# Retention values and gates of two heads as one 2x2 block product by seven products, with six blocks of branch gates made early and kept in DRAM

## The chip, the cores and the metric

One core of one Trainium2 chip runs the whole program. The metric is the time of one execution on the device in microseconds (us), median of several runs. TensorE is called PE here, VectorE DVE, ScalarE ACT, GpSimd POOL, and SyncE, whose queue issues every DMA of this kernel, SP.

## What is computed

Two layers of an encoder run over 512 tokens of width 1024. Each layer projects its input `x` by `w_in` into queries and keys of three branches, into values, into a retention gate and into three branch gates; mixes tokens by retention (A), chunked attention (B) and differential attention (C); adds the three branches under sigmoid gates; and ends with an output projection, a layer norm, a SwiGLU feed-forward part and a second norm.

```python
h = jnp.einsum('bsd,de->bse', x, w_in[l])
rq, rk, rv, rg, cq, ck, cv, dq, dk, dv, gates = jnp.split(h, splits, axis=-1)
o_a = _retention(rq, rk, rv, rg, ret_norm_g[l])
...
g = jax.nn.sigmoid(gates + b_merge[l]).reshape(B, S, N_BRANCHES, D)
merged = g[:, :, 0] * (o_a @ w_branch_a[l]) + g[:, :, 1] * (o_b @ w_branch_b[l]) + g[:, :, 2] * (o_c @ w_branch_c[l])
```

The change concerns `rv` and `rg` (1024 columns each, in two halves of 512 that serve two heads each) and `gates` (three branches of 1024 columns).

## The kernel before, in words

**Numbers.** Every float32 operand is held as a pair of float32r tiles, a high part and the remainder (`Pair`, `split`). A product of two such operands is three matmuls, high by high, high by low, low by high (`mm3`, L106 to L108). A weight block of 1 MB is loaded into a stage (`st`, three buffers), then ACT casts the high part (`wh`, L135) and DVE subtracts to get the low part (`wl`, L136), in two pieces each; there are three such pairs of weight buffers (`AHEAD`), so weights are prepared up to three blocks ahead of PE. All other tiles of 128x512 share one pool of 60 slots (`NSLOT`). [...]

**Order of the work.** A layer is a list of items, each a weight block (or some of them) and a function that issues its matmuls (L902 and on, and after it the output projection and the feed-forward items). `run_items` (L440) fetches weights ahead. Between the products of an item `between` (L434) issues steps of the attention branches: `s_r1` to `s_r3` for retention, `c(i)` (L887) for the chunked attention, `d(i)` for the differential attention. The framework then schedules the instructions of each engine into one static queue; an instruction waits at the head of its engine's queue for semaphores, and everything behind it waits with it.

**Start of a layer.** `u_first` (L562) projects the first queries and keys for retention. In the first layer (`whole`) eight tiles of x arrive one by one beside the first weight block, and 48 matmuls of two banks run in the order in which they arrive; then come two more weight blocks (96 matmuls). At its end it calls `vectors` (L491): seven small DMAs bring biases and norm weights as rows into one tile `rows`, PE transposes it into `pcol` (L503), ACT copies it to `colv`, and DVE makes `hb`, half the gate bias, from it. Before all this PE runs 16 transposes on the identity (L462).

**Values and gates.** `u_rv` (L555) and `u_rg` (L593) each take two weight blocks of 512 columns and make four token tiles in natural layout, `pn`, each by 8 k-tiles x 3 = 24 matmuls of 512 columns: 96 for `rv` and 96 for `rg` of one pair of heads. `u_gate(br, i)` (L855) makes two gate tiles (48 matmuls), ACT takes their tanh, and they stay in SBUF until the next item, `u_branch(br, i)` (L866), multiplies a branch's projection by them. The gates of branch A stand directly ahead of their branch, as do those of B; those of C are the last items ahead of C's branch.

**Feed-forward output.** Its first 16 k-tiles are done as 2x2 block products by seven products instead of eight (`Halves`, L142, loads and adds the weight blocks; `Quarters`, L212, the sums of the activations; `fout_items`, L1028), each product interleaved with a 48-matmul item of the feed-forward input.

**Norm.** At the end of a layer `Norm.to_T` (L405) makes the transposed input of the next one: ACT applies the norm's weights into a passing tile `lnt` (L414), and `split` makes the pair.

Of the kernel before, what the change touches and what calls it, by code (L numbers as in the profile page):

```python
# [43 lines left out]
NSLOT = 60  # L44
# [9 lines left out]
def trunk(ctx, tc, x_in, xT_in, w_in, ret_norm_g, da_norm_g, lq1, lk1, lq2, lk2, w_a, w_b, w_c, b_merge, w_out,  # L54
# [87 lines left out]
    class Halves:  # L142
# [6 lines left out]
        def __init__(self, w, r0, kh):  # L149
            self.w, self.r0, self.kh = w, r0, kh  # L150

        def load(self, i, j, tag="st", **kw):
            t = wst.tile([P, 2048], F32, tag=tag, name=tag, **kw)[:, :512 * self.kh]
            t = t.rearrange("p (k c) -> p k c", k=self.kh)
            r = P * (self.r0 + i * self.kh)
            nc.sync.dma_start(t, self.w[r:r + P * self.kh, 512 * j:512 * j + 512].rearrange("(k p) c -> p k c", p=P))
            return t
# [54 lines left out]
    class Quarters:  # L212
# [3 lines left out]
        def __init__(self, t1, t2, scale=None):  # L216
            a, b = slice(0, 256), slice(256, 512)
# [11 lines left out]
            self.use = {"m1": (q[:, a], q[:, b])}  # L229
            for names, pr in ((("m2", "h"), p2), (("y", "x"), p12), (("v", "g"), p43)):  # L230
                for name, sl in zip(names, (a, b)):
                    self.use[name] = (pr.hi[:, sl], pr.lo[:, sl])
# [119 lines left out]
    class Norm:  # L352


        def __init__(self, z, gcol, bcol, gam, bet, xT, dst):
            self.__dict__.update(z=z, gcol=gcol, bcol=bcol, gam=gam, bet=bet, xT=xT, dst=dst)
            self.st = [small.tile([P, 2, 6], F32, tag="bn", name="bn") for _ in range(NT)]
            self.banks = {}
# [46 lines left out]
        def to_T(self, hf, ks=range(KT)):  # L405
            cols = slice(256 * hf, 256 * hf + 256)
            for k in ks:
# [3 lines left out]
                if self.gcol is not None:  # L411
                    t = g(name="lnt")[:, :256]
                    gc, bc = self.gcol[:, k:k + 1], self.bcol[:, k:k + 1]
                    nc.scalar.activation(t, src, AF.Identity, scale=gc, bias=bc)  # L414
                    src = t
                split(self.xT[k], src, cols=cols)
# [47 lines left out]
    start = {}  # L464

    def load_x(k0, k1):
        for k in range(k0, k1):
            start[k] = g(name="xn")
            nc.sync.dma_start(start[k], xT_in[P * k:P * k + P])

    def split_x(k0, k1):
        for k in range(k0, k1):
            xTs[0][k] = Pair("xT")
            src, pr = start.pop(k), xTs[0][k]
# [3 lines left out]
    xTs = [[None] * KT for _ in range(DEPTH + 1)]  # L478
    hooks = {}

    def layer(l):
        lambda_init = 0.8 - 0.6 * math.exp(-0.3 * l)
        xT = xTs[l]
# [65 lines left out]
        def rv_part(hp, wts, t):  # L549
            ps = bank("pn")  # L550
            proj_N(xT, wts, t, ps)
            rv[hp, t] = Pair("rv")
            split(rv[hp, t], ps)

        def u_rv(hp):  # L555
            def fn(*wts):
                for t in range(NT):
                    rv_part(hp, wts, t)
                    between()
            return rows_of(W, RV + 512 * hp), fn  # L560

        def u_first():  # L562

            dst = [(rq, 0), (rk, 0), (rq, 2)]

            def whole(*wts):
                ret_tables()
                banks = [bank("pt") for _ in range(2)]
# [4 lines left out]
                for w, (d, h) in zip(wts, dst):  # L573
                    for j in range(2):
                        rqk_done(d, h + j, banks[j] if w is wts[0] else proj_T(xT, w, P * j))
                vectors()

            def halves(*wts):
                ret_tables()
                banks = [[bank("pt") for _ in range(2)] for _ in wts[:2]]  # L580
# [4 lines left out]
                for w, p, (d, h) in zip(wts, banks, dst):  # L585
                    for j in range(2):
                        rqk_done(d, h + j, proj_T(xT, w, P * j, ps=p[j], half=1))
                vectors()

            fn = whole if l == 0 else halves  # L590
            return [([wcols(c, 256)], KT) for c in (RQ, RK, RQ + 256)], fn

        def u_rg(hp):  # L593
            def fn(*wts):
                for t in range(NT):
                    ps = bank("pn")
                    proj_N(xT, wts, t, ps)
# [4 lines left out]
                    between()  # L602
            return rows_of(W, RG + 512 * hp), fn
# [250 lines left out]

        def u_gate(br, i):  # L855
            def fn(wt):
                for j in range(2):
                    d = 2 * i + j
                    ps = proj_T(xT, wt, P * j)
                    t = g(name="th")  # L860
                    nc.scalar.activation(t, ps, AF.Tanh, scale=0.5, bias=v["hb"][:, 8 * br + d:8 * br + d + 1])
                    th[br, d] = t
# [3 lines left out]
        def u_branch(br, i):  # L866
# [3 lines left out]
            def fn(wt):  # L870
                act = (oa, ob, oc)[br]
                for j in range(2):
                    d = 2 * i + j
                    ps = proj_T(act, wt, P * j, nk=nk)
                    t = th.pop((br, d))
# [25 lines left out]

# [293 lines left out]
```

## Time and profile before

| | |
|---|---|
| median of 3 runs | 1943.55 us (1943.06 to 1944.1) |
| the profiled execution's own time | 1943.5 us |
| its span, first to last instruction | 1941.7 us |
| mean granted clock of PE | 0.998 |
| PE busy | 1928.8 us (99%), 9346 matmuls |
| DVE busy | 1189.0 us (61%) |
| ACT busy | 846.2 us (44%) |
| DMA | 214 MB on the SP queue |

The 1.8 us between the span and the execution's own time lie outside the recorded instructions. A page of the profile gives busy times by engine, the span in 40 slices, the chain of work that ended last, and groups of instructions by source line with their mean duration. Durations of neighbouring matmuls overlap, as the array is a pipeline; what a matmul costs is the distance between the starts of two neighbours, which the timeline view shows.

### The profile page before, as it was taken

The numbers are of one execution on the slowest core, as the hardware profiler recorded it, in microseconds if no ns is written. First come the engines' busy times: TensorE is split into PE (matmuls) and PEld (weight loads), VectorE is DVE, ScalarE is ACT, GpSimd is POOL, SyncE is SP. The second block draws the span as 40 slices with busy tenths as digits, with TensorE's granted clock in tenths as the row PEclk, the third lists the DMA queues.
The fourth block names the chain that finished last, engine by engine and source line by source line (L and its number), as shares of the span: only waits on it lengthen the run. The fifth ranks groups of instructions, "written<-read, shape, count | busy, mean of one in ns | idle before, by whom it ended". The sixth has DMA issues, their size and how long they took to land. (4 is left out here: it accounts for less than half of the span.)

```text
span 1941.7 us, 23842 instructions
## 1 busy us (share of the span) xinstructions
PE 1928.8 (99%) x9346; PEld 1624.6 (84%) x9346; DVE 1189.0 (61%) x2022; ACT 846.2 (44%) x1511; POOL 44.4 (2%) x73
## 2 busy tenths in 40 slices
PE   9999999999999999999999999999999999999998
PEld 7888888888888888888898888888888888888886
DVE  7455556577556766656576545655775567675666
ACT  5334455466534333333254344555674343332330
POOL 0000000000000000000000000000000000000000
PEclk9999999999999999999999999999999999999999
DMA  7232332232244443434343223222221624444341
GB/s 256 94 102 66 99 102 88 70 98 77 66 160 123 131 152 114 146 107 141 122 163 99 76 87 103 79 90 87 87 87 44 207 76 152 131 151 131 102 130 50
DMA packets 228533, 215.78 MB, mean 111 GB/s; under 512 B 7118, under 2 KB 179268, under 8 KB 228420
## 3 DMA queue, kind: packets, MB, share of 16 engines
q1 hardware_dynamic: 228420, 214.26, 35.2%
q8 instruction: 73, 1.20, 0.3%
q14 instruction: 40, 0.33, 0.1%
HBM read 205.84 MB, written 8.39 MB: 110 GB/s over the span
## 5 line engine op out<-in xcount | busy, mean ns | idle before, releaser
L106 PE MATMUL pt<-xTh,wh 128*128 128x512 f32 (+1 forms) x1584 | 596.8, 377 | 1.2 <-ACT xTh L475 1.1
L107 PE MATMUL pt<-xTl,wh 128*128 128x512 f32 (+1 forms) x1584 | 593.8, 375 | 1.1 <-DVE xTl L476 1.1
L108 PE MATMUL pt<-xTh,wl 128*128 128x512 f32 (+1 forms) x1584 | 593.2, 375 | 0.0
L136 DVE TENSOR_TENSOR wl<-st,wh 128x1024 fp32r<-128x1024 f32 (+1 forms) x314 | 353.3, 1144 | 176.7 <-ACT wh L135 176.6
L135 ACT CAST wh<-st 128x1024 fp32r<-128x1024 f32 (+1 forms) x314 | 301.6, 989 | 324.6 <-PE pt L107 162.3
L107 PEld LDWEIGHTS pt<-xTl,wh 128*128 128x128 f32 x1584 | 298.7, 189 | 54.4 <-DVE xTl L476 2.3
L106 PEld LDWEIGHTS pt<-xTh,wh 128*128 128x128 f32 x1584 | 298.5, 189 | 54.4 <-ACT xTh L475 2.4
L108 PEld LDWEIGHTS pt<-xTh,wl 128*128 128x128 f32 x1584 | 298.4, 188 | 53.7
L106 PE MATMUL pn<-wh,xTh 128*128 128x512 f32 x384 | 150.8, 393 | 0.0
L107 PE MATMUL pn<-wl,xTh 128*128 128x512 f32 x384 | 149.6, 390 | 0.0
L108 PE MATMUL pn<-wh,xTl 128*128 128x512 f32 x384 | 149.6, 390 | 0.0
L985 DVE TENSOR_TENSOR fth<-fth,pt 128x512 f32<-128x512 f32 x44 | 30.2, 686 | 115.6 <-PE pt L108 115.6
L108 PEld LDWEIGHTS pn<-wh,xTl 128*128 128x128 f32 x384 | 72.1, 188 | 15.2
L106 PEld LDWEIGHTS pn<-wh,xTh 128*128 128x128 f32 x384 | 72.1, 188 | 14.2
L107 PEld LDWEIGHTS pn<-wl,xTh 128*128 128x128 f32 x384 | 72.2, 188 | 14.0
L983 ACT ACTIVATE fth<-pt 128x512 f32<-128x512 f32 x44 | 26.3, 599 | 124.4 <-PE pt L108 124.4
L271 ACT COPY sw<-pt 32x512 f32<-32x512 f32 (+1 forms) x96 | 55.7, 580 | 31.4 <-PE pt L108 30.1
L984 DVE SCALAR_TENSOR_TENSOR fth<-fth,pt 128x512 f32<-128x512 f32 x44 | 30.1, 683 | 58.9 <-ACT fth L983 58.9
L209 ACT CAST wh<-st 128x1024 fp32r<-128x1024 f32 x32 | 32.1, 1051 | 74.4 <-PE pt L107 74.4
L106 PE MATMUL pt<-oah,wh 128*128 128x512 f32 x128 | 50.9, 397 | 0.0
L108 PE MATMUL pt<-oah,wl 128*128 128x512 f32 x128 | 50.0, 390 | 0.0
L107 PE MATMUL pt<-oal,wh 128*128 128x512 f32 x128 | 49.9, 390 | 0.0
(232 smaller groups left out, 2979.3 us busy)
## 6 DMA issues: line engine op xcount, KB each, us to landing
st<-in_w_in SPq DMA_DIRECT2D x55, 1024.0 KB
st<-in_w_ffn_in SPq DMA_DIRECT2D x88, 512.0 KB
st<-in_w_ffn_out SPq DMA_DIRECT2D x28, 1024.0 KB
st<-in_w_in SPq DMA_DIRECT2D x32, 512.0 KB
st<-in_w_branch_a SPq DMA_DIRECT2D x8, 1024.0 KB
st<-in_w_out SPq DMA_DIRECT2D x8, 1024.0 KB
saved<-z SPq DMA_DIRECT2D x24, 256.0 KB
z<-saved SPq DMA_DIRECT2D x24, 256.0 KB
```

The source lines that it names most:

```text
L106: nc.tensor.matmul(ps, lh, rh, start=start, stop=False)
L107: nc.tensor.matmul(ps, lh, rl, start=False, stop=False)
L108: nc.tensor.matmul(ps, ll, rh, start=False, stop=stop)
L135: done = [nc.scalar.copy(self.hi[:, a:b], st[:, a:b]), nc.vector.tensor_sub(self.lo[:, a:b], st[:, a:b], f(self.hi[:, a:b]))]
L136: nc.vector.tensor_sub(self.lo[:, a:b], st[:, a:b], f(self.hi[:, a:b]))]
L209: nc.scalar.copy(self.hi[:, s], st[:, s])
L271: nc.scalar.copy(sw[half * b:half * b + half], ps[half * o:half * o + half])
L983: nc.scalar.activation(t, pg, AF.Tanh, scale=0.5)
L984: nc.vector.scalar_tensor_tensor(t, t, 1.0, pg, op0=ALU.add, op1=ALU.mult)
L985: nc.vector.tensor_mul(t, t, pu)
```

## The change

For each pair of heads, `rv` and `rg` together (512 tokens by 1024 columns, 1024 deep) become one 2x2 block product by seven products, in the manner of the feed-forward output: `u_rvg` makes seven items `m1`, `y`, `x`, `m2`, `v`, `g`, `h`, each of one weight block of 512x512 and 2 x 4 x 3 = 24 matmuls of 512 columns. Four of the seven weight blocks are sums or differences made by DVE (`t1` to `t4`), and DVE also adds the products together. The activations' sums need x in float32, so x's tiles (`xf`, in the second layer written by `to_T`) stay until `s_q` has made the sums of four k-pairs. `u_first` takes the first gate block of branch A in place of the second block of queries, so `vectors`, which gives the gate bias, moves ahead of the first matmuls in both layers. Six gate blocks (`EARLY`: all four of A, two of C) stand between the seven products, leave SBUF to DRAM tiles and come back in the branch items. The steps of retention and of chunked attention move to other places in the list; `c(i)` now falls into nearly every item from the first branch on. `NSLOT` is 61. The feed-forward's `Quarters` is split into `parts` and `sums`, and `t4` adds where it subtracted, with the sign moved to its user.

In the built program the counts change so: matmuls of 512 columns from 7464 to 7368, other PE instructions not at all; DVE gains 32 instructions of 256 columns, 72 of 512 and 56 of 1024; ACT gains 32 of 512 and 24 of 1024; SP gains 60 DMAs and 25.2 MB.

```diff
+EARLY = [(0, 0), (0, 1), (0, 2), (0, 3), (2, 0), (2, 1)]
+
+NSLOT = 61
...
-        def __init__(self, w, r0, kh):
-            self.w, self.r0, self.kh = w, r0, kh
+        def __init__(self, w, r0, kh, cols=(0, 512)):
+            self.w, self.r0, self.kh, self.cols = w, r0, kh, cols
...
-            b, a = self.load(1, 0), self.__dict__.pop("a")
-            for s in self.parts():
-                nc.vector.scalar_tensor_tensor(b[:, s], a[:, s], -1.0, b[:, s], op0=ALU.mult, op1=ALU.subtract)
+            b = self.load(1, 0)
+            self.add(b, self.__dict__.pop("a"))
...
+    def product(acts, name, j, wt):
+
+        ps, sl = bank("pf"), slice(P * j, P * j + P)
+        for k in range(wt.nk):
+            hi, lo = acts[k].use[name]
+            mm3(ps, hi[:, sl], lo[:, sl], wt.hi[:, k], wt.lo[:, k], k == 0, k == wt.nk - 1)
+        return ps
 
...
+        def sums(self, t1, t2, scale=None):
+            a, b = self.A, self.B
             sa, sb = g(name="sa"), g(name="sb")
             nc.vector.tensor_sub(sa[:, a], t1[:, b], t2[:, b])
             nc.vector.tensor_sub(sa[:, b], t1[:, a], sa[:, a])
             nc.vector.tensor_sub(sb[:, a], t2[:, a], sa[:, b])
             nc.vector.tensor_sub(sb[:, b], t1[:, b], t1[:, a])
-            q, p2, p12, p43 = g(F32R, "q11"), Pair("q2"), Pair("s12"), Pair("s43")
-            part_hi(q[:, a], t1[:, a], scale)
-            part_lo(q[:, b], t1[:, a], q[:, a], scale)
-            split(p2, t2, scale=scale)
...
+                    if k not in self.rows:
+                        self.rows[k] = g(name="xf")
+                    t = self.rows[k][:, cols]
...
+            def done(i, j, ps):
+                if (i, j) == (0, 0):
+                    xq.update({k: Quarters(xT[k], xT[k + 4]) for k in range(4)})
+                if i < 2:
+                    rqk_done((rq, rk)[i], j, ps)
+                else:
+                    gate_done(0, j, ps)
 
             def whole(*wts):
                 ret_tables()
+                vectors()
                 banks = [bank("pt") for _ in range(2)]
                 for k in range(KT):
                     for j in range(2):
                         a, c = xT[k], slice(P * j, P * j + P)
                         mm3(banks[j], wts[0].hi[:, k, c], wts[0].lo[:, k, c], a.hi, a.lo, k == 0, k == KT - 1)
-                for w, (d, h) in zip(wts, dst):
+                for i, w in enumerate(wts):
                     for j in range(2):
-                        rqk_done(d, h + j, banks[j] if w is wts[0] else proj_T(xT, w, P * j))
-                vectors()
+                        done(i, j, proj_T(xT, w, P * j) if i else banks[j])
 
             def halves(*wts):
                 ret_tables()
+                vectors()
                 banks = [[bank("pt") for _ in range(2)] for _ in wts[:2]]
                 proj_T_half0(xT, [(w, P * j, p[j]) for w, p in zip(wts, banks) for j in range(2)], {})
                 banks.append([bank("pt") for _ in range(2)])
                 proj_T_half0(xT, [(wts[2], P * j, banks[2][j]) for j in range(2)],
                              {2 * b: functools.partial(hooks[l], b) for b in range(4)})
-                for w, p, (d, h) in zip(wts, banks, dst):
+                for i, (w, p) in enumerate(zip(wts, banks)):
                     for j in range(2):
-                        rqk_done(d, h + j, proj_T(xT, w, P * j, ps=p[j], half=1))
-                vectors()
+                        done(i, j, proj_T(xT, w, P * j, ps=p[j], half=1))
 
             fn = whole if l == 0 else halves
-            return [([wcols(c, 256)], KT) for c in (RQ, RK, RQ + 256)], fn
-
-        def u_rg(hp):
-            def fn(*wts):
-                for t in range(NT):
-                    ps = bank("pn")
-                    proj_N(xT, wts, t, ps)
-                    s = g(name="rg")
-                    nc.scalar.activation(s, ps, AF.Tanh, scale=0.5)
-                    nc.vector.scalar_tensor_tensor(s, s, 1.0, ps, op0=ALU.add, op1=ALU.mult)
-                    rgt[hp, t] = s
-                    between()
-            return rows_of(W, RG + 512 * hp), fn
+            return [([wcols(c, 256)], KT) for c in (RQ, RK, GATE)], fn
...
+            hv = Halves(W, 0, 4, (RV + 512 * hp, RG + 512 * hp))
...
+            def x(j, ps):
+                u, y = g(name="tu"), t["y", j]
+                t["u", j] = u
+                nc.vector.tensor_sub(u, ps, t["m", j])
+                nc.vector.tensor_add(y, y, u)
+
+            def m2(j, ps):
+                c = t.pop(("m", j))
+                nc.vector.tensor_add(c, c, ps)
+                rv_done(hp, j, c)
+
+            def v(j, ps):
+                c = g(name="tv")
+                nc.vector.tensor_add(c, t["y", j], ps)
+                rg_done(hp, j, c)
+
+            def g_(j, ps):
+                c, u = t.pop(("y", j)), t["u", j]
+                nc.vector.tensor_add(c, c, ps)
+                nc.vector.tensor_add(u, u, ps)
+                rg_done(hp, 2 + j, c)
+
+            def h(j, ps):
+                u = t.pop(("u", j))
+                nc.vector.tensor_sub(u, ps, u)
+                rv_done(hp, 2 + j, u)
+
+            return {"m1": it(hv.b11, "m1", copy("m")), "y": it(hv.t1, "y", copy("y")), "x": it(hv.t2, "x", x),
+                    "m2": it(hv.b21, "m2", m2), "v": it(hv.b22, "v", v), "g": it(hv.t3, "g", g_),
+                    "h": it(hv.t4, "h", h)}
...
+        def gate_done(br, d, ps, away=True):
+            t = g(name="th")
+            nc.scalar.activation(t, ps, AF.Tanh, scale=0.5, bias=v["hb"][:, 8 * br + d:8 * br + d + 1])
+            th[br, d] = t
+            if away:
+                th[br, d] = dram.tile([P, 512], F32, name=f"th{l}_{br}_{d}")
+                nc.sync.dma_start(th[br, d], t)
+
+        def gate_of(br, d):
+            t = th.pop((br, d))
+            if (br, d // 2) in EARLY:
+                away, t = t, g(name="th")
+                nc.sync.dma_start(t, away)
+            return t
+
...
+                ts = [gate_of(br, 2 * i + j) for j in range(2)]
...
+        p, q = u_rvg(0), u_rvg(1)
         for (specs, fn), *groups in [
-            (u_first(),), (u_rv(0), [], [], [s_r1(0)], []), (u_rg(0), [], [], [s_r1(1)], [s_r2(0)]),
-            (u_rqk(rk, RK, 1), [], [s_r3(0)]),
-            (u_rv(1), [s_r2(1)], [], [s_r3(1)], [s_r1(2)]), (u_rg(1), [], [s_r1(3)], [], []),
-            (u_vhl(cv, CV, 64), [s_r2(2)], [s_r2(3)], [s_r3(2)], [s_r3(3)]), (u_cqk(0),),
-            (u_gate(0, 0), *c(0)), (u_branch(0, 0), *c(1)), (u_cqk(1),),
-            (u_gate(0, 1), *c(2)), (u_branch(0, 1), *c(3)), (u_cqk(2),),
-            (u_gate(0, 2), *c(4)), (u_branch(0, 2), *c(5)), (u_cqk(3),),
-            (u_gate(0, 3), *c(6)), (u_branch(0, 3), *c(7)),
-            (u_vhl(dv, DV, 128), *c(8), *c(9)), (u_dqk(0),),
+            (u_first(),), (u_gate(0, 1), [s_q(0)], [s_q(1)]), (p["m1"], [], [s_q(2)]),
+            (u_gate(0, 2), [s_q(3)], [s_r1(0)]), (p["y"],), (p["x"],), (u_gate(0, 3), [], [s_r1(1)]), (p["m2"],), (p["v"],),
+            (u_gate(2, 0),), (p["g"],), (p["h"],),
+            (u_rqk(rq, RQ, 1), [], [s_r2(0)]), (q["m1"],), (u_rqk(rk, RK, 1), [s_r2(1)], [s_r3(0)]), (q["y"], [], [s_r3(1)]),
+            (u_gate(2, 1),), (q["x"],), (q["m2"],), (q["v"],), (q["g"],), (q["h"],),
+            (u_vhl(cv, CV, 64), [s_r1(2)], [s_r1(3)], [s_r2(2)], [s_r2(3)]), (u_cqk(0), [s_r3(2)], [s_r3(3)]),
+            (u_branch(0, 0), *c(0)), (u_cqk(1), *c(1)), (u_branch(0, 1), *c(2)), (u_cqk(2), *c(3)),
+            (u_branch(0, 2), *c(4)), (u_cqk(3), *c(5)), (u_branch(0, 3), *c(6)),
+            (u_vhl(dv, DV, 128), *c(7), *c(8)), (u_dqk(0), *c(9)),
             (u_gate(1, 0), *d(0)), (u_branch(1, 0), *d(1)), (u_dqk(1),),
             (u_gate(1, 1), *d(2)), (u_branch(1, 1), *d(3)), (u_dqk(2),),
             (u_gate(1, 2), *d(4)), (u_branch(1, 2), *d(5)), (u_dqk(3),),
-            (u_gate(1, 3), *d(6)), (u_branch(1, 3), *d(7)), (u_gate(2, 0), [s_d4(2)], [s_d2(3)]),
-            (u_gate(2, 1), [], [s_d3(3)]), (u_gate(2, 2), [], [s_d4(3)]), (u_gate(2, 3),),
+            (u_gate(1, 3), *d(6)), (u_branch(1, 3), *d(7)), (u_gate(2, 2), [s_d4(2)], [s_d2(3)]),
+            (u_gate(2, 3), [s_d3(3)], [s_d4(3)]),
             (u_branch(2, 0),), (u_branch(2, 1),), (u_branch(2, 2),), (u_branch(2, 3),),
```

The first instructions of PE's queue in the built program, in the first layer, are these, where `pcol` stood behind the 144 matmuls of `u_first` before:

```
warm <- ident, ident         16 transposes
pcol <- ident, rows          1 transpose, waits for the DMAs of rows
pt <- xTh, wh                first of the 144 matmuls of u_first
```

More of the change, by code (lines that the diff above doesn't have):

```diff
@@ L410, in to_T @@
                 src = self.banks[hf][k // 2][:, 256 * (k % 2):256 * (k % 2) + 256]
-                if self.gcol is not None:
+                if self.rows is None:
                     t = g(name="lnt")[:, :256]
[L413 to L416, printed above, removed]
+                else:
+                    if k not in self.rows:
+                        self.rows[k] = g(name="xf")
+                    t = self.rows[k][:, cols]
+                nc.scalar.activation(t, src, AF.Identity, scale=self.gcol[:, k:k + 1], bias=self.bcol[:, k:k + 1])
+                split(self.xT[k], t, cols=cols)
         def natural(self, t):
@@ L478, in trunk @@
     xTs = [[None] * KT for _ in range(DEPTH + 1)]
+    xfs = [{} for _ in range(DEPTH + 1)]
     hooks = {}
```

105 lines of the change are left out of this document (62 added, 43 removed).

## The prediction

> **What bounds the kernel now.** First the page: the busy times, then the chain that ended last.
>
> ```profile
> span 1941.7 us, 23842 instructions
> PE 1928.8 (99%) x9346; PEld 1624.6 (84%) x9346; DVE 1189.0 (61%) x2022; ACT 846.2 (44%) x1511; POOL 44.4 (2%) x73
> ...
> q1 hardware_dynamic: 228420, 214.26, 35.2%
> ...
> DVE 1%; issue 0%; DVEq 0%
> ```
>
> The chain names only a tail on DVE, so I go by stretches. The windows view (length, then busy us by engine, granted clock, DMA share, GB/s) shows whether PE ever waits once it runs:
>
> ```profile
> 25.00:200.00 175.00, 175.00 (x859) 148.11 (x858) 93.81 (x149) 70.88 (x130) 5.30 (x7) 1.00 0.35 115
> 200.00:600.00 400.00, 400.00 (x1928) 335.69 (x1928) 243.36 (x494) 208.97 (x418) 11.39 (x18) 1.00 0.31 97
> ```
>
> It doesn't: PE fills both. From 25 us on time is the number of matmuls times their spacing, which is read from the starts in PE's timeline (start, duration), not from their overlapping durations:
>
> ```profile
> 139.45 0.39 PE L108 MATMUL pn<-wh,xTl 128*128 128x512 f32 x1
> ...
> 141.49 0.39 PE L108 MATMUL pn<-wh,xTl 128*128 128x512 f32 x1
> ```
>
> Nine spacings take 2.04 us: **0.2267 us** for a matmul of 512 columns. The only stretch with holes is the start:
>
> ```profile
> 1.48 3.68 PE L462 MATMUL warm<-ident 128*128 128x128 f32 x16 [1.48 <-POOL ident masks.py:199]
> 5.10 0.80 PE L106 MATMUL pt<-xTh,wh 128*128 128x512 f32 x1
> ...
> 17.52 0.50 PE L106 MATMUL pt<-xTh,wh 128*128 128x512 f32 x1 [1.12 <-ACT xTh L475]
> ...
> 20.08 0.63 PE L108 MATMUL pt<-xTh,wl 128*128 128x512 f32 x1
> ...
> 22.64 0.59 PE L108 MATMUL pt<-xTh,wl 128*128 128x512 f32 x1
> 23.06 0.40 PE L106 MATMUL pt<-xTh,wh 128*128 128x512 f32 x1
> ```
>
> PE runs its first matmuls as x's tiles land: the row at 20.08 is the 48th, and by 23.06 54 have started. Their spacing from 20.08 to 22.64 is 0.427 us (2.56 over six), not 0.227.
>
> **What goes.** Per layer and pair of heads 96 + 96 matmuls become 7 x 24 = 168. Two pairs, two layers: 4 x 24 = 96 matmuls fewer, all of 512 columns, and no other PE instruction less or more. 96 x 0.2267 = **-21.8 us**, since PE is never idle there.
>
> **What moves: the start.** In the built queue of PE the transpose of `rows` (`pcol`) now stands ahead of the first matmul. PE is in order, so all 144 matmuls of `u_first` wait until the last of the seven `rows` DMAs has landed. SP's own order up to there is unchanged: x and three weight blocks first. When it issues the last two of the seven is in SP's timeline:
>
> ```profile
> 18.86 0.27 SPq L499 DMA_DIRECT2D rows<-in_ln_g  x1
> 19.18 0.30 SPq L499 DMA_DIRECT2D rows<-in_ln_b  x1
> ```
>
> They can't land before 19.48. For the other end I ask the DMA view for 20.6 to 22.0 us; a row of `rows` is a packet of 512 bytes (128 floats):
>
> ```profile
> DMA packets 230, 0.05 MB, mean 38 GB/s; under 512 B 230, under 2 KB 230, under 8 KB 230
> ```
>
> No packet of 512 bytes is left, so the last landed between 19.5 and 20.6. I take 20.6, adding nothing for the semaphore. What follows it:
>
> ```profile
> 43.28 0.39 PE L108 MATMUL pt<-xTh,wl 128*128 128x512 f32 x1
> 43.60 0.28 PE L503 MATMUL pcol<-ident,rows 64*128 64x64 f32 x1
> 43.81 0.50 PE L106 MATMUL pn<-wh,xTh 128*128 128x512 f32 x1
> ```
>
> 0.2 us after `pcol` the next matmul starts, so with 0.1 us to release the wait the first one starts at 20.9 us instead of 5.10. The cover is gone: ACT and DVE, which split x and the weights meanwhile, no longer run beside matmuls. (In the second layer the same DMAs are issued during the first and cost nothing; `pcol`'s old place returns 0.53 - 0.23 = 0.3 us.)
>
> How slow is PE then? The windows view again, over stretches of 3.41 us, with the clock in the third column from the end:
>
> ```profile
> 5.99:9.41 3.42, 3.22 (x12) 2.00 (x12) 2.01 (x4) 2.37 (x4) 0.00 (x0) 1.00 1.00 350
> ...
> 16.23:19.65 3.42, 1.46 (x5) 0.86 (x5) 2.68 (x3) 2.96 (x4) 0.00 (x0) 1.00 0.92 304
> 19.65:23.06 3.41, 3.41 (x9) 2.63 (x8) 3.40 (x5) 2.37 (x4) 0.00 (x0) 0.50 0.11 27
> ```
>
> PE was busy 94% of the first and kept its clock after it; 43% of the second, and the clock was 0.50 for the next 3.41 us; after a full one it came back. In the changed kernel PE idles from 5.2 to 20.9, so it starts at half clock, 0.427 us a matmul. If it gets its clock back at 23.06, as here, 5 matmuls have run by then, and it is 54 - 5 = 49 matmuls behind: 49 x 0.2267 = **+11.1 us**. The upper end is one more half-clock window, 3.41 / 2 = 1.7 us: +12.8. The stretch up to 23.06 would be 63% busy (2.16 of 3.41), between the 43% that lost the clock and the 94% that kept it, and where these stretches begin in another execution isn't known: I take the middle, **+11.9**. The lower end, with `rows` landing at 19.5, is +10.0.
>
> [...]
>
> **What is added beside PE.** Rows by form (count, busy us, mean ns):
>
> ```profile
> L136 DVE TENSOR_TENSOR wl<-st,wh 128x1024 fp32r<-128x1024 f32 x270 | 324.0, 1219 | 107.4 <-ACT wh L135 107.3
> L135 ACT CAST wh<-st 128x1024 fp32r<-128x1024 f32 x270 | 275.7, 1050 | 258.5 <-PE pt L107 120.7 <-issue 87.2 <-PE pf L108 23.2
> L1024 DVE TENSOR_TENSOR z<-z,pf 128x512 f32<-128x512 f32 x60 | 39.9, 680 | 12.0 <-PE pf L108 12.0
> L219 DVE TENSOR_TENSOR sa<-fth 128x256 f32<-128x256 f32 x16 | 6.8, 424 | 0.5
> ```
>
> DVE: 56 x 1.22 + 72 x 0.68 + 32 x 0.42 = 131 us more, 1320 of some 1934 (68%). ACT: 24 x 1.05 and 32 copies of about 0.6 = 45 us. SP: 60 DMAs, 239 MB instead of 214, or 39% at the present rate. None becomes the bound by its sum. I cost them at nothing where PE's matmuls cover them, and look at the three tightest places.
>
> (1) The second pair's last five products, `x m2 v g h`, follow each other. PE: 5 x 24 x 0.2267 = 27.2 us. DVE: ten half-block splits and six half-block sums, 16 x 1.22 = 19.5, and 14 additions and 8 gate or value steps of 512, 22 x 0.68 = 15.0 (`x` and `g` four additions each): 34.5 us, 7.3 more than PE. Buffers let DVE run two products (10.9 us) ahead, so 7.3 fit, if it comes in time; and back to back it is faster than its means say:
>
> ```profile
> 971.91 3.49 DVE L136 TENSOR_TENSOR wl<-st,wh 128x1024 fp32r<-128x1024 f32 x3
> ```
>
> 1.16 each, not 1.22. I take 0.
>
> (2) `y` of the first pair stands right behind a gate item, and its last k-pair's sum, queued behind that item's freed weight buffer (one cast of 1.05, two DVE halves of 1.22, the sum's low part), is due 11 matmuls (2.5 us) after 1.9 us of retention scores: 1.05 + 2 x 1.2 + 0.7 = 4.2 against 4.4. It meets, barely.
>
> (3) At the end of the mixer two gate items instead of four stand between the last steps of branch C. After `s_d3` one gate product, 24 x 0.2267 = 5.4 us, covers what took here:
>
> ```profile
> 1491.33 0.22 PE L821 MATMUL pdo<-vhl,dPl 128*128 128x128 f32 x1
> ...
> 1502.38 0.60 PE L846 MATMUL pdt<-ident,do 128*128 128x128 f32 x4
> ```
>
> ```profile
> 1495.42 0.87 DVE L836 TENSOR_SCALAR do<-do,rsr 128x128 f32<-128x128 f32 x4 [1.12 <-POOL rsr L833]
> ...
> 1504.21 0.75 DVE L98 SCALAR_TENSOR_TENSOR ocl<-pdt,colv,och 128x512 fp32r<-128x512 f32 x1 [0.47 <-ACT och L92]
> ```
>
> 1491.33 to 1496.29 is 5.0 us, so it fits by 0.4. Then `ocl` was ready 2.6 us after `pdt` began, and the first branch product needs it after 0.4 + 11 x 0.2267 = 2.9. It fits by 0.3.
>
> Places (2) and (3) have margins below half a microsecond, in both layers. Bounds: 0, and some 6 us if DVE or ACT come a microsecond and a half late at each of the four; a loss only, as PE can't gain. I take **+1.4**, near the lower end, because the rows fit. The gates from DRAM are waited for by DVE, with PSUM banks to spare, and are issued before their branch's matmuls: 0.
>
> **Sum**, against the profiled execution's 1943.5 us (span 1941.7 and 1.8 around it; the median, 1943.55, is the same): 1943.5 - 21.8 - 0.3 + 11.9 + 1.4 = **1934.7 us**. The start gives back half of what the seven products save.
>
> **The rivals.**
>
> *The start is hidden* (6%). If `rows` landed by 5 us, or PE's queue had the transpose elsewhere, the 11.9 goes: 1922.8. Against it: SP issues them at 19 us, behind x and three weight blocks, 5 MB.
>
> [...]
>
> *The denser chunked attention makes ACT late* (10%). A `c` step came with two of three items and now comes with nearly each. Beside a query-key item ACT has:
>
> ```profile
> L323 ACT ACTIVATE cE<-cE,mx 128x512 f32<-128x512 f32 x16 | 11.6, 724 | 15.4 <-DVE mx L321 15.4
> L92 ACT ACTIVATE qs<-pt 64x512 fp32r<-64x512 f32 x16 | 9.5, 593 | 26.1 <-PE pt L108 19.8 <-DVE qs L98 6.3
> L90 ACT CAST ks<-pt 64x512 fp32r<-64x512 f32 x32 | 18.6, 582 | 10.7 <-PE pco L746 10.3
> ```
>
> 2 x 0.593 + 4 x 0.582 + 2 x 1.05 for the item and about 6 for the step (exponentials of 0.72 and less, casts of 0.6, reads): 11.6 us against 10.9 of matmuls and some 3 of the step's own. An in-order ACT at 80% makes transposes wait; at 0.7 us in each of 7 items and 2 layers it is +9.8: 1944.5, within 0.2%. For 2 of 3 items the trace shows no such wait.
>
> *DVE enters the five products late* (8%). The place is the second pair's `x` to `h`; it decides by what DVE has in hand of its 10.9 us when they begin. With less than 7.3, PE waits for the difference; with less than 2.9 (4.4 us lost, in two layers 8.8, the margin of the sum) the kernel is slower than before; with nothing in hand it is 2 x 7.3 = 14.6 on top: 1949.3. Against it: gate items of 10.9 us, beside which DVE has two splits (2.4 us), stand close ahead.
>
> **How the numbers follow.** The forecast has 52%: its own range is 1931 (`rows` at 19.5, clock back at once, no loss at the margins) to 1939.5 (a loss of 6 at the margins). With the half-clock window that is 76%. The range reaches from there into ACT late and leaves out the hidden start (6%), DVE late (8%) and the upper part of ACT late: **1931 to 1942**. A measurement of this kernel tells about 0.2% (3.9 us) from no change. Faster by more (below 1939.7): 52 + 24 + 6 = 82%. Within 0.2%: 10%. Slower: 8%.
>
> **What would show it.** In the profile after: PE's first 512-column matmul near 20.9 us, behind `pcol`, with a wait on the `rows` DMA; the clock at 0.50 up to 23 or 26.5; 9250 matmuls; from 30 us on PE full in every window, and the products (`pf` on `xTh`, `s12h`, `s43h`) spaced 0.227. Wrong if the first matmul is at 5 us, or if PE's idle after 30 us is above some 3 us, named by DVE `wl` or sums (the products) or by ACT (the attention).

## The result and the profile after

| | before | after |
|---|---|---|
| median of 6 runs, us | 1943.3 (1941.14 to 1944.1) | 1950.12 (1948.44 to 1952.43) |
| profiled execution, us | 1943.5 | 1950.65 (span 1948.8) |

The ratio is **1.0037**, with a 95% interval of 1.0025 to 1.005: 6.8 us slower, where 8.8 us faster was forecast. The page of the changed kernel has the 9250 matmuls of the forecast and the queue's 239 MB, and no engine near its bound but PE:

```profile
span 1948.8 us, 24029 instructions
PE 1910.1 (98%) x9250; PEld 1608.0 (83%) x9250; DVE 1305.7 (67%) x2182; ACT 885.9 (45%) x1567; POOL 44.3 (2%) x73
...
q1 hardware_dynamic: 241668, 239.43, 38.8%
```

PE was busy 18.7 us less than before (1910.1 against 1928.8) and the span is 7.1 longer, so PE waits. Where, the windows view tells (length; busy us of PE, PEld, DVE, ACT, POOL; clock, DMA share, GB/s):

```profile
30.00:215.00 185.00, 185.00 (x861) 154.89 (x861) 134.32 (x182) 89.26 (x135) 2.04 (x2) 1.00 0.47 154
260.00:400.00 140.00, 134.02 (x658) 111.11 (x657) 83.94 (x193) 73.31 (x154) 3.12 (x6) 0.99 0.28 89
400.00:1190.00 790.00, 789.71 (x3877) 668.75 (x3876) 550.80 (x864) 360.18 (x607) 13.59 (x20) 1.00 0.41 131
1200.00:1400.00 200.00, 194.41 (x970) 162.25 (x969) 126.21 (x278) 108.72 (x231) 8.26 (x14) 1.00 0.30 95
```

The seven products of the first layer lie in the first of these windows, and PE is full there: they cost nothing beside their matmuls. PE idles in the chunked attention of both layers, where the kernel before was full (its window 200 to 600, shown ahead; in the second layer, from 1000 to 1400 us, it is full too). The start is the other place. PE's timeline (start, duration; in brackets the wait and what ended it):

```profile
21.72 0.34 PE L535 MATMUL pcol<-ident,rows 64*128 64x64 f32 x1 [16.57 <-DMA rows<-in_ln_b]
21.99 0.79 PE L109 MATMUL pt<-xTh,wh 128*128 128x512 f32 x1
...
27.28 0.40 PE L109 MATMUL pt<-xTh,wh 128*128 128x512 f32 x1
```

The first product starts at 21.99 us behind `pcol`, as forecast, 1.1 us later than forecast; SP issued the last load of `rows` later too:

```profile
20.01 0.30 SPq L531 DMA_DIRECT2D rows<-in_ln_b  x1
```

**Holes.** For a count in us I take the starts of all 9250 matmuls and add up what each spacing has over its normal value (0.2267 us behind one of 512 columns, and so on for shorter ones). An example, from PE's timeline in the attention:

```profile
299.37 0.39 PE L111 MATMUL pt<-oah,wl 128*128 128x512 f32 x1
301.25 0.50 PE L824 MATMUL pco<-cPh,vhl 128*128 128x512 f32 x1 [1.49 <-ACT cPh L93]
```

The spacing is 1.88, the hole 1.65. The sums (what a half clock costs counts in them; "attention" is 215 to 400 and 1100 to 1400 us, both layers; differences in the text are taken before rounding):

| profiled execution | start, 0 to 28 us | attention | all the rest |
|---|---|---|---|
| before | 7.6 | 1.9 | 4.9 |
| after | 21.3 | 18.5 | 3.6 |

So -21.8 (96 matmuls) + 13.7 (start) + 16.5 (attention) - 1.3 (rest) = +7.1 us, the difference of the two profiled executions (1950.65 - 1943.5).

**What PE waits for in the attention.** The chain of one step, first from SP (issues), then on ACT. L789 loads the bias tile `tb`, L790 negates it, L352 are the exponentials, L93 the casts of the keys and of the transposed probabilities `cPh`, L138 the weights':

```profile
286.05 0.38 SPq L132 DMA_DIRECT2D st<-in_w_branch_a  x1
286.47 0.58 SPq L789 DMA_DIRECT2D tb<-in_rel  x1
```

```profile
292.17 0.63 ACT L790 ACTIVATE tb<-tb 128x512 f32<-128x512 f32 x1 [3.72 <-DMA tb<-in_rel]
293.86 0.72 ACT L352 ACTIVATE cE<-cE,mx 128x512 f32<-128x512 f32 x1 [1.06 <-DVE mx L350]
...
296.18 1.17 ACT L93 CAST ks<-pt 64x512 fp32r<-64x512 f32 x2
297.38 2.00 ACT L138 CAST wh<-st 128x1024 fp32r<-128x1024 f32 x2
299.41 1.17 ACT L93 CAST ks<-pt 64x512 fp32r<-64x512 f32 x2
300.61 1.35 ACT L93 CAST cPh<-ptr 128x512 fp32r<-128x512 f32 x3
```

`tb` is issued 0.42 us behind a weight block of 1 MB on the same queue and can be used 5.7 us later. ACT, which takes its queue in order, stands for 3.72 us, stands for 1.06 more until DVE's `mx` is there, and then does without a pause what has come due meanwhile; the cast of `cPh` starts at 300.61, and PE, at `pco`, has stood since 299.76. The kernel before had the same load. In the same stretch (SP, then ACT) it was issued 2.15 us behind a weight block and not 0.42:

```profile
281.26 0.37 SPq L129 DMA_DIRECT2D st<-in_w_in  x1
283.41 0.34 SPq L711 DMA_DIRECT2D tb<-in_rel  x1
```

```profile
287.08 0.63 ACT L712 ACTIVATE tb<-tb 128x512 f32<-128x512 f32 x1 [2.03 <-DMA tb<-in_rel]
```

3.7 us from issue to use. It is so with the loads of `tb` that ACT waited for in the two kernels' attention. With a weight block issued at most 0.9 us ahead of them they took 4.8 to 5.7 us from issue to use, in before as in after, and 4.7 with the block 1.0 or 1.1 us ahead (before); with reloads of gates right between a block and them 5.3 to 6.5 (after); with the block more than 2 us ahead and no reload between 3.3 to 3.7 (before), and with the block 9.0 and 7.7 us ahead 3.1 and 3.5, though reloads stood between (after, issued at 368.74 and 1328.64). The view of waits (total us, times, longest), after from 260 to 400 us, then before from 200 to 380, a stretch of about as many steps:

```profile
ACT tb L790 <- DMA tb<-in_rel: 28.3, 8, 5.6
DVE tb L791 <- ACT tb L790: 17.8, 8, 3.7
...
DVE th L966 <- DMA th<-th: 7.6, 3, 3.6
...
PEld pco L824 <- ACT cPh L93: 6.1, 3, 2.5
```

```profile
DVE tb L713 <- ACT tb L712: 17.1, 7, 5.4
ACT tb L712 <- DMA tb<-in_rel: 15.5, 7, 3.6
```

Before waited for `tb` as well, and PE felt nothing of it. So a late `tb` alone is not enough; what it takes is the question of the experiments.

### The profile page after: what moved, and what is told of

It reads as the page before. It is cut to its first block, busy times and chain, and to the rows that moved or that the text cites. A ratio compares the mean times of both kernels' runs of the same rounds, so it can differ in the third digit from the quotient of the medians.

```text
span 1948.8 us, 24029 instructions
## 1 busy us (share of the span) xinstructions
PE 1910.1 (98%) x9250; PEld 1608.0 (83%) x9250; DVE 1305.7 (67%) x2182; ACT 885.9 (45%) x1567; POOL 44.3 (2%) x73
## 5 line engine op out<-in xcount | busy, mean ns | idle before, releaser
L138 ACT CAST wh<-st 128x1024 fp32r<-128x1024 f32 (+1 forms) x282 | 268.2, 982 | 276.6 <-issue 122.9
L139 DVE TENSOR_TENSOR wl<-st,wh 128x1024 fp32r<-128x1024 f32 (+1 forms) x282 | 313.5, 1135 | 103.5 <-ACT wh L138 103.4
L212 ACT CAST wh<-st 128x1024 fp32r<-128x1024 f32 x64 | 65.2, 1051 | 98.9 <-PE pt L110 64.9
L213 DVE TENSOR_TENSOR wl<-st,wh 128x1024 fp32r<-128x1024 f32 x64 | 76.6, 1220 | 8.8 <-ACT wh L212 8.6
L212 ACT CAST wh<-sa 128x1024 fp32r<-128x1024 f32 x48 | 49.5, 1050 | 66.8 <-PE pt L110 62.5
L213 DVE TENSOR_TENSOR wl<-sa,wh 128x1024 fp32r<-128x1024 f32 x48 | 57.8, 1219 | 21.0 <-ACT wh L212 21.0
L109 PE MATMUL pn<-wh,xTh 128*128 128x512 f32 x128 | 50.4, 394 | 0.0
L109 PE MATMUL pf<-wh,s12h 128*128 128x512 f32 x128 | 50.0, 391 | 0.0
L111 PE MATMUL pn<-wh,xTl 128*128 128x512 f32 x128 | 49.9, 390 | 0.0
```

The source lines that it names most:

```text
L109: nc.tensor.matmul(ps, lh, rh, start=start, stop=False)
L111: nc.tensor.matmul(ps, ll, rh, start=False, stop=stop)
L138: done = [nc.scalar.copy(self.hi[:, a:b], st[:, a:b]), nc.vector.tensor_sub(self.lo[:, a:b], st[:, a:b], f(self.hi[:, a:b]))]
L139: nc.vector.tensor_sub(self.lo[:, a:b], st[:, a:b], f(self.hi[:, a:b]))]
L212: nc.scalar.copy(self.hi[:, s], st[:, s])
L213: nc.vector.tensor_sub(self.lo[:, s], st[:, s], f(self.hi[:, s]))
```

## The experiments

The theories for the attention: **A**, ACT stands at the negation of `tb`, and only because the negation is ACT's; **C**, the gates' reloads from DRAM do it (slots, queue, DVE's waits for `th`); **D**, the steps are too dense for ACT and DVE in any case; **F**, formed after the first four runs, `tb`'s landing is late whatever engine uses it first, and the dense steps have no time to spare for that. For the start the theory is `pcol`'s place in PE's queue, against **B**, that PE's late start is made good by 30 us anyway. **E** is that the seven products themselves cost PE time. (In the expectations of e1, e4 and e7, A stands for the theory of the start too.) In the expectations the holes are counted from 260 to 400 and 1200 to 1400 us (9.8 and 8.4 after, 0.6 and 0.9 before); in this table as above. The median of before beside these runs was 1943.1 (the first eight) and 1943.3.

| kernel | median us | ratio to before, 95% interval | start | attention |
|---|---|---|---|---|
| after, vectors behind 96 matmuls (e1) | 1935.29 | 0.9963, 0.9948 to 0.9977 | 7.1 | 19.3 |
| after, negation on DVE (e2) | 1948.34 | 1.0031, 1.0019 to 1.0044 | 19.0 | 18.6 |
| after, no stores and reloads of gates (e3) | 1944.07 | 1.0005, 0.9996 to 1.0015 | 19.2 | 13.7 |
| e1 and e2 (e4) | 1933.54 | 0.9953, 0.9938 to 0.9967 | 5.7 | 16.6 |
| after, `tb` a step ahead (e5) | 1936.56 | 0.9968, 0.9955 to 0.9981 | 21.0 | 5.8 |
| e1 and e5 (e6) | 1924.4 | 0.9904, 0.9889 to 0.9919 | 8.0 | 5.8 |
| before, vectors early (e7) | 1955.7 | 1.0066, 1.005 to 1.0081 | 19.6 | 1.8 |
| before, dense steps (e8) | 1953.22 | 1.0053, 1.0036 to 1.007 | 6.0 | 12.4 |
| e6, reloads an item ahead (e9) | 1924.92 | 0.9906, 0.9889 to 0.9922 | 7.3 | 6.3 |
| e8, `tb` a step ahead (e10) | 1944.0 | 1.0007, 0.9997 to 1.0016 | 5.9 | 4.3 |

Part of these holes is half clock, by estimate 1.7 us for each window of 3.41 us at 0.50 (3.41 x 0.50; the last section). In the start, sums of 7.1 to 8.0 have one such window and those of 5.7 to 6.0 none. In the attention there is one in after, e1, e2, e3 and e4, two in e8, and none in before, e5, e6, e7, e9 and e10.

**e1: the vectors back behind matmuls.**

```
                 ret_tables()
-                vectors()
                 banks = [bank("pt") for _ in range(2)]
...
                 for i, w in enumerate(wts):
+                    if i == 2:
+                        vectors()
                     for j in range(2):
```

> The changed kernel with one thing undone: in the first layer the vectors (the seven small row loads, the transpose pcol and what follows) stand in front of the third block of the first item, the gates, instead of in front of its first matmul. Theory A (the loss is the start, some 13.7 us, and ScalarE held up in the chunked attention, some 16.7 us): first matmul back near 5 us, 13 to 14 us less than the changed kernel, 1936 to 1938; the holes of the attention stay as they are. Theory B (PE's late start is made good later anyway, because the weights' splitting or the loads set the pace up to 30 us): less than 5 us gained, 1945 to 1950.

1935.29, 14.8 less than after and 0.7 below the range expected. PE's first product is back at 5.18 us, the start's holes at 7.1; the attention keeps its holes. The start's theory holds, and B falls.

**e2: the negation on DVE.**

```
-                nc.scalar.mul(tb, tb, -1.0)
+                nc.vector.tensor_scalar_mul(tb, tb, -1.0)
```

> The changed kernel with the negation of the bias tile tb in the chunked attention moved from ScalarE to VectorE (18 instructions); the load, its place and everything else as they are. Theory A (ScalarE, in order, stands at that negation until the tile's load lands, and the casts behind it come late for TensorE): ScalarE's wait for tb goes, holes of TensorE at 260 to 400 and 1200 to 1400 us fall from 9.8 and 8.4 us to below 3 each, 12 to 16 us less, 1934 to 1938. Theory C (the reloads of the gates from DRAM take slots and queue time, and the softmax steps come late whatever engine negates): the holes stay within 2 us of what they are, VectorE waits in place of ScalarE, 1947 to 1951. Theory D (the density of the c steps itself overloads ScalarE): at most 2 to 4 us gained, since 20 negations of some 0.6 us are 12 us of ScalarE work and only part of it counts.

1948.34: A falls. The waits, from 260 to 400 us:

```profile
ACT cE L352 <- DVE mx L350: 30.8, 7, 7.3
...
DVE tb L790 <- DMA tb<-in_rel: 12.4, 8, 2.9
```

ACT now stands as long (30.8 us) at the exponential, which is next in its queue and needs the same `tb` through DVE's `mx`. Who negates makes no difference to the attention (18.6 against 18.5); the 1.8 us less lie in the start.

**e3: no gates through DRAM.**

```
-                th[br, d] = dram.tile([P, 512], F32, name=f"th{l}_{br}_{d}")
-                nc.sync.dma_start(th[br, d], t)
+                th[br, d] = None
...
-                away, t = t, g(name="th")
-                nc.sync.dma_start(t, away)
+                t = g(name="th")
+                nc.gpsimd.memset(t, 0.5)
```

> The changed kernel without the way of the six gate blocks through DRAM: their 24 stores and 24 reloads are left out, and the branch takes a constant 0.5 in their place, written by GpSimd (the gates are still computed, then dropped; tiles and slots as before). Theory A: the tb loads come a little earlier at most, as SP's queue is shorter: 0 to 5 us less, 1945 to 1950. Theory C (the reloads are what makes the attention late): the holes at 260 to 400 and 1200 to 1400 us go, 14 to 17 us less, 1933 to 1936.

This kernel leaves the values of the six blocks' gates out: the branch takes a constant 0.5. 1944.07, 6.1 less: between the two. Of the 7.1 between the profiled executions (1950.65 and 1943.58) the start accounts for 2.1 (19.2 against 21.3, a matter of the clock and of when `rows` came, below), the attention for 4.8. So the reloads are a part, under a third of the 16.5 us, and not the main cause.

**e4: e1 and e2 together.**

> Both edits on the changed kernel: the vectors of the first layer behind the first 96 matmuls, and the negation of tb on VectorE. Theory A: the two gains add up to 25 to 30 us, 1920 to 1925, that is the 21.8 us of the seven products below the kernel before. Theory D or C: 1933 to 1937, as only the start comes back. Theory E (the seven products themselves cost TensorE time that the other holes hide so far): 1926 or more although the holes are gone.

1933.54: only the start comes back, as D or C had it. After these four, two things stood side by side that were not told apart: `tb` late, and dense steps.

**e5: `tb` one step ahead.** The step of head h issues the load of head h + 1; all else stays, the negation on ACT too.

```
...
+        def load_tb(h):
+            tbs[h] = tb = g(name="tb")
+            src = rel[l, h:h + 1, 0:1]
+            nc.sync.dma_start(tb, bass.AP(src.tensor, src.offset, [[1, P], [1, 512]]))
...
+                if h == 0:
+                    load_tb(h)
+                if h + 1 < CA_HEADS:
+                    load_tb(h + 1)
+                tb = tbs.pop(h)
```

> The changed kernel with the bias tile tb of a chunked-attention head loaded one step earlier (at the step of the head before); the negation is back on ScalarE. Theory F (tb's load, some 5.5 us from issue to landing because it is issued right behind a weight block on the same queue, is late whatever engine uses it first; ScalarE and VectorE, in order, then come late with the casts): the waits for tb go, holes of TensorE at 260 to 400 and 1200 to 1400 us fall from 9.8 and 8.4 us to 4 together or less, 13 to 17 us less than the changed kernel, 1933 to 1937. Theory D (the steps are too dense for ScalarE and VectorE even with tb there): the waits for tb go, but half or more of the holes stay, 1942 or more. Theory C (the reloads of the gates from DRAM): at most 5 to 6 us less, as without the reloads, 1944 or more.

1936.56, 13.6 less than after. The holes of the attention fall from 18.5 to 5.8. The `tb` that is used at 291.90 was issued with its forerunner at 272.80 (SP, then ACT):

```profile
272.80 0.90 SPq L790 DMA_DIRECT2D tb<-in_rel  x2
```

```profile
291.90 0.63 ACT L799 ACTIVATE tb<-tb 128x512 f32<-128x512 f32 x1
```

No wait stands behind this one any more. Not all of them are gone, as the expectation had it; the first head's load still comes with its own step (waits from 260 to 400 us):

```profile
ACT tb L799 <- DMA tb<-in_rel: 10.1, 3, 5.8
```

10.1 us against after's 28.3, and the holes, counted as in the expectations, are some 5.5 us and not 4. F holds for the most part; of D at most the 3.8 us that remain over before's 1.9 can be true.

**e6: e1 and e5 together.**

> The same early tb load together with the vectors behind the first 96 matmuls. Theory F: both losses gone, 1919 to 1923, the 21.8 us of the seven products below the kernel before, and 0 to 3 us of holes. Theory D: 1928 or more, as with the vectors alone (1935) less half of the holes.

1924.4, 1.4 above F's range, since 5.8 us of holes remain and not up to 3. E falls: the time is below its 1926. It is the best version of the study, 18.7 us (1.0%) faster than before and 25.7 faster than after. Its windows over the attention:

```profile
215.00:400.00 185.00, 184.46 (x930) 154.51 (x929) 115.19 (x249) 99.37 (x210) 8.27 (x14) 1.00 0.31 97
1100.00:1400.00 300.00, 299.50 (x1481) 251.54 (x1481) 202.78 (x390) 165.81 (x336) 10.52 (x17) 1.00 0.35 109
```

So the seven products bring their 21.8 us: -21.8 + 0.4 (start) + 3.8 (attention) - 1.1 (rest) = -18.7.

**e7: before with the vectors early.** In `whole` of the kernel before, `vectors()` stands ahead of the banks and no longer behind the loop.

> The kernel before with one thing of the change done: in the first layer the vectors stand in front of the first matmul. Theory A (the start costs by the place of pcol alone): first matmul near 21 to 22 us, 11 to 14 us more, 1954 to 1957, everything behind 30 us as in the kernel before. Rival: the gates as third block, which need the vectors sooner, or the longer SP queue are part of it, so less here: 1945 to 1952.

1955.7, 12.6 more, with the attention's holes as they were (1.8): `pcol`'s place alone. Its transpose started at 20.28.

**e8: before with dense steps.**

```
-            (u_gate(0, 0), *c(0)), (u_branch(0, 0), *c(1)), (u_cqk(1),),
-            (u_gate(0, 1), *c(2)), (u_branch(0, 1), *c(3)), (u_cqk(2),),
...
+            (u_gate(0, 0), *c(0)), (u_cqk(1), *c(1)), (u_branch(0, 0), *c(2)), (u_cqk(2), *c(3)),
+            (u_gate(0, 1), *c(4)), (u_cqk(3), *c(5)), (u_branch(0, 1), *c(6)),
+            (u_gate(0, 2), *c(7)), (u_branch(0, 2), *c(8)), (u_gate(0, 3), *c(9)), (u_branch(0, 3),),
...
```

> The kernel before with its chunked-attention steps as close as in the changed kernel: one in each item, the query-key items among them, no seven products, no gates from DRAM, the vectors where they were. Theories F and D (density is what makes tb and the casts late): holes of 5 to 9 us in each layer in the stretch of the attention, 10 to 17 us more, 1953 to 1960, with waits for tb in the view of waits. Theory C (the reloads make it): no holes, 1942 to 1945.

1953.22, 10.1 more, at the low end of what was expected: holes of 12.4 with none of the seven products, no reload and no early vector. Two half-clock windows (from 232.57 and 1201.96 us) make some 3.4 of them. The same rows as in after show the same chain (SP, then ACT):

```profile
216.32 0.37 SPq L129 DMA_DIRECT2D st<-in_w_branch_a  x1
216.74 0.57 SPq L711 DMA_DIRECT2D tb<-in_rel  x1
```

```profile
222.23 0.63 ACT L712 ACTIVATE tb<-tb 128x512 f32<-128x512 f32 x1 [3.80 <-DMA tb<-in_rel]
...
230.66 1.35 ACT L90 CAST cPh<-ptr 128x512 fp32r<-128x512 f32 x3
```

Why density matters can be read from such rows, after's above for one: in a query-key item the four casts `ks` and the next weights' casts stand in front of `cPh` too, and `cPh` starts 8.4 us behind `tb` (300.61 and 292.17; here 8.4 too). In the kernel before, where no step was put into such an item, it started 4.7 us behind (291.73 and 287.08), and `pco` began only at 296.69: ACT could lose up to 3.6 us at `tb` and be in time. That it is the query-key items, and not the closeness of the steps in general, no run tried by itself.

**e9: e6 with the reloads of branch A's gates one item ahead.** The reload is issued at the start of `u_cqk(p)`.

> The kernel with the vectors late and tb one step early (1924.4 us), and now the reloads of branch A's gates from DRAM also one item earlier, at the start of the query-key item ahead of their branch item. If the reloads still hold VectorE up (6.0 us of waits for th in the stretch of the attention) and so TensorE: the holes left there, 2.2 and 2.7 us, fall to 1 each, 1921 to 1923. If those waits are covered, or the slots taken earlier cost as much: 1924 to 1926, holes within 0.5 us of what they were.

1924.92, and 6.3 us of holes against 5.8: nothing gained, although DVE's waits for `th`, 6.0 us in e6 from 260 to 400 us, are gone. They were covered once `tb` was a step ahead.

**e10: e8 with `tb` one step ahead.** The edits of e8 and e5 on the kernel before.

> The kernel before with the dense chunked-attention steps (1953.2 us, holes of 13 us in all from 215 to 400 and 1100 to 1400 us), and tb one step early. Theory F (density hurts through tb's load alone, by its place behind a weight block on the queue): the holes fall to 4 or less in all, 1942 to 1946. Theory D (ScalarE and VectorE are too full when the steps are this close): half or more stays, 1948 or more.

1944.0, 9.2 less than e8 and within 0.2% of before; the holes are 4.3 and not quite the 4 expected. Its waits, from 190 to 330 us, beside those of e8 from the same stretch:

```profile
ACT tb L721 <- DMA tb<-in_rel: 6.5, 3, 3.5
```

```profile
ACT tb L712 <- DMA tb<-in_rel: 19.1, 8, 3.8
```

So, in holes above before's 1.9, dense steps with `tb` a step ahead cost 2.4 us, a late `tb` with loose steps nothing (before), and both together 10.5 (e8). After, without the reloads, has 11.8 (e3), and with them on the same queue 16.5.

## Why the prediction was wrong

- **What goes: right.** 96 matmuls at 0.2267 us; the products run without a hole, and e6 has the whole gain.
- **The three tight places: nothing lost, where +1.4 had been put.** Outside the start and the attention no single hole is above 0.2 us, but for one of 0.45 in each layer that before has too (ahead of `px`); all the rest of the span has 1.3 us less of holes than before.
- **The start: right in mechanism, mis-sized by 1.8 us.** 13.7 against 11.9 and an upper end of 12.8 (e7, without the rest of the change, has 11.9 in holes and 12.6 in the medians). `rows` was issued 0.8 us later, as `20.01` against `19.18` shows, and the first product began at 21.99 and not 20.9. From that issue to the first product the prediction had 1.7 us, with 0.1 for the release of the wait, which no run shows by itself; the five kernels with early vectors have 2.0 to 2.3. And the half clock lasted up to 27.27 (the windows below): the last term was a middle between two cases, and the profiled execution had the worse, one more half-clock window (24% in the forecast, 12.8 in place of 11.9, 1935.6 us in all). How near a middle comes is luck: e2, e3 and e5 have the same start, and theirs cost 11.4, 11.6 and 13.4 us more than before's, with `rows` issued at 18.38, 18.85 and 19.38. The lower end of +10.0 is a slip; a first product at 19.8 gives 7.6 matmuls by 23.06 and so +10.5.
- **The gates from DRAM at 0: wrong by about 5 us.** They were looked at for what waits for them (DVE's `th`); that PSUM had banks to spare for that wait, no run shows by itself. Without them the attention's holes are 4.8 us smaller (e3), and once `tb` comes a step ahead their own wait costs nothing (e9). They stood in front of `tb`, as after's rows show (SP, then ACT):

```profile
301.27 0.98 SPq L945 DMA_DIRECT2D th<-th  x2
302.36 0.61 SPq L789 DMA_DIRECT2D tb<-in_rel  x1
```

```profile
308.00 0.63 ACT L790 ACTIVATE tb<-tb 128x512 f32<-128x512 f32 x1 [3.37 <-DMA tb<-in_rel]
```

In e3 the same load, as far behind its weight block (1.50 us) but with no reload between, could be used 4.4 us after its issue and not 5.6:

```profile
299.47 0.34 SPq L789 DMA_DIRECT2D tb<-in_rel  x1
```

```profile
303.84 0.63 ACT L790 ACTIVATE tb<-tb 128x512 f32<-128x512 f32 x1 [2.08 <-DMA tb<-in_rel]
```

- **The step that failed: costing what is beside PE at nothing, but for three tight places.** The chunked attention was not among them; it stood as a rival, "the denser chunked attention makes ACT late", at 10% and +9.8 us. Its holes are 16.5 of the some 16 us by which the profiled execution missed the forecast; the start (+1.8) and the rest (-2.4) nearly cancel. So the rival's place came true, and the prediction's own sign of being wrong with it (PE idle after 30 us, named by ACT in the attention), but at another price and not by its mechanism, an ACT too busy. The rival's working compared ACT's busy time in an item (11.6 us) with PE's (10.9 and 3), which made it look like a matter of 0.7 us. A sum of busy time does not see that ACT can't begin: it stood 28.3 us in that stretch at a tile still under way. The row that says so was in the trace of before, 15.5 us of ACT's waits for `tb`, but it was never asked what those waits would do if the items that made them good were filled up. "For 2 of 3 items the trace shows no such wait" was true of PE and not of ACT.

Not settled: what the 3.8 us of holes in e6's attention over before's come from. The largest single ones are 0.43 us; ACT still waits 9.6 us for `tb` there from 260 to 400 us, 5.7 of them for the first head's.

## What to carry to other kernels

When steps are moved closer together, look at what the in-order engines wait for in the old profile, not only at how busy they are: a wait on a load that costs nothing today is slack that the new order may spend. Ask of each load which larger one stands ahead of it on its queue (`tb` took 5.7 us from issue to use 0.42 us behind a block, 3.7 us 2.15 us behind one), and issue small ones a step early; that was worth 12.7 us of the 16.5 here. And ask of every instruction that moves forward in a queue whether its data is there: a transpose of 64 rows held up 144 matmuls, with PE idle for 16.57 us (after).

## What the runs showed of the clock and of the queue

Five kernels started PE after a long idle (16.57 us in after, 14.96 in e2, 15.42 in e3, 15.98 in e5, 15.25 in e7). In each the full clock came back behind 3.41 us in which PE was busy throughout: from 23.86 us in after, 20.72 in e2, 23.92 in e5 and 21.85 in e7; in e3 it was back between 24.00 and 24.28, and PE was busy from 20.59. The windows ahead of these, 63% (after), 18% (e2), 82% (e5) and 46% (e7) busy, did not bring it back. The windows view of after, from the instant at which the clock came back, and then of e5 (the clock's column has no record ahead of 27.27 and shows 1.00 there; the spacing of 0.427 us shows the half clock, and 0.50 in the second row is the DMA's share):

```profile
20.44:23.86 3.42, 2.14 (x5) 1.67 (x6) 2.99 (x5) 1.47 (x3) 0.20 (x1) 1.00 0.11 27
23.86:27.27 3.41, 3.41 (x9) 2.64 (x8) 0.30 (x3) 0.00 (x0) 0.00 (x0) 1.00 0.50 163
27.27:30.69 3.42, 3.42 (x16) 2.82 (x15) 0.55 (x3) 0.20 (x1) 0.00 (x0) 1.00 1.07 378
```

```profile
20.51:23.92 3.41, 2.78 (x7) 2.21 (x8) 2.31 (x4) 0.76 (x2) 0.20 (x1) 1.00 0.11 28
```

63% busy and even 82% were not enough: in after nine matmuls in the following full window, sixteen in the one after it. So the middle taken in the prediction was too kind to this start. Where `pcol` came 1.6 us earlier (e2, at 20.12) a full window began 0.6 us later and the clock was back at 24.13: the start's holes are 19.0 there and 21.3 in after, the spread that such a start has of itself.

The other way, a hole of 2.2 us in the attention cost the clock where it fell into one window, and didn't where two windows shared it (after, first layer, then second layer):

```profile
361.77:365.19 3.42, 1.37 (x7) 0.83 (x6) 2.15 (x5) 2.24 (x5) 0.00 (x0) 1.00 0.26 90
365.19:368.61 3.42, 3.42 (x14) 2.94 (x13) 1.27 (x3) 0.27 (x1) 0.00 (x0) 0.50 0.32 101
```

```profile
1320.92:1324.34 3.42, 2.88 (x13) 2.06 (x11) 2.24 (x8) 1.85 (x5) 0.00 (x0) 1.00 0.49 153
1324.34:1327.75 3.41, 1.91 (x11) 1.69 (x12) 2.32 (x4) 2.18 (x5) 0.00 (x0) 1.00 0.04 10
```

40% busy lost it for the next 3.41 us (at 0.50, by estimate a further 1.7 us of work); 84% and 56% kept it. 43% lost it in before (16.23 to 19.65 us, shown ahead), and 40% in e1 (1309.41 to 1312.82). In between the share alone doesn't decide. 49% lost it in e6 (0.50 from 20.43 us), and 48% kept it in e1 (1.00 from 350.27):

```profile
17.02:20.43 3.41, 1.67 (x6) 1.18 (x7) 3.05 (x4) 2.97 (x5) 0.00 (x0) 1.00 0.68 229
```

```profile
346.86:350.27 3.41, 1.65 (x8) 1.03 (x6) 2.17 (x6) 1.83 (x4) 0.00 (x0) 1.00 0.43 145
```

The small load was in use 5.7 us after its issue where it stood 0.42 us behind the larger one on SP's queue (after), and 3.7 us after it where it stood 2.15 us behind (before). Whether another queue would have spared it the 2 us was not shown: no run here issued `tb` from one.
